# RWKV-7 recurrence of a two-network kernel: chunks of 64 tokens in place of chunks of 32

## Chip, core and metric

One core of one Trainium2 chip runs the whole program in one launch. The metric is the device time in microseconds (us). The kernel before takes 2678.37 us, the median of three runs (2671.02 to 2682.64).

## The reference, cut to what matters

Two small networks run one after the other on 256 latent and 256 context tokens of width 1024. Most of the work is matrix products with weights that stream from HBM. The change is in one part of the first network, the RWKV-7 recurrence of its even mixer: 8 heads of 64 features, two directions, and in each direction the 256 context tokens come first and hand their final state to the 256 latent tokens.

```
def step(S, inp):                       # S: [heads, 64 values, 64 keys]
    r, w, k, v, kk, a = inp             # one token
    S = (S * w[:, :, None, :]
         - jnp.einsum('bhvk,bhk->bhv', S, kk)[..., None] * (kk * a)[:, :, None, :]
         + v[..., None] * k[:, :, None, :])
    return S, jnp.einsum('bhvk,bhk->bhv', S, r)
S, y = lax.scan(step, S0, xs, reverse=reverse)
```

Token by token this is 512 dependent steps. In chunks it becomes products: inside a chunk the term in `kk` couples each token to the earlier ones, which needs the inverse of a triangular matrix 1 + N (N strictly triangular, as wide as the chunk) for each head and direction; between chunks only the state S is handed on.

## The kernel before

Names: d is the direction, m one of four pairs of heads, par the head within a pair, J a block of work. Features stand on partitions, so a pair of heads fills 128 partitions, 64 for each head.

`features` (L815) makes, for all tokens, `ARw` (alpha, rho: what multiplies the state) and `BKw` (kappa, beta: what goes into it), each with the decay from the chunk's start, and `EC`, the decay over the chunk before. It runs beside the global attention and ends at 664.9 us. Then the recurrence goes in 8 blocks of two chunks of 32 tokens, for both directions at once.

`prepare(J)` (L909) does what needs no state: products G of `BKw` and `ARw` (L922); N is cut from them (L928) and masked (L933); the causal mask gives the lower half of `AR` (L941), and `ARw` times the decay its upper half (L963); `BKw` is transposed to `TM` (L946, L950). Then the inverse `Z` of all 32 triangles (two directions, four pairs, four quadrants of 32 partitions for head and chunk) is made in two levels of three steps each, a step being 32 products of 32x32 blocks (L976) and one or two VectorE operations for each direction (L979 to L995). `Z` is written at L995.

`chain(J)` (L1001) takes the two chunks of the block one after the other. A tile `VS` holds for each head the state on its own 64 partitions and V and U on the other 64, so one product over all 128 partitions does for state and chunk together: R = `AR` (alpha) on `VS` (L1015), copied to `rs` (L1017); U = `Z` times `rs` (L1021), copied to `VS` in four pieces, in turns on VectorE and ScalarE (L1024); the new state from `TM` and V, U (L1028), plus the decayed old one (L1034, L1035); and the outputs Y (L1040), copied or added to `rt` (L1045, L1047).

`weave` runs `chain(J)` and two steps of `prepare(J + 1)` in turns, and a scheduler then sets the order in each engine's queue. A queue is taken in that order: an instruction that waits holds up all behind it. The last block is woven with the output projection (`ending`, and `out_split`).

All of these products are float32 and use part of TensorE's 128x128 array: the trace writes the part as rows*columns (64*64, 128*64, 32*32), and `tile_position` in the code says where in the array it stands. The trace shows two records for each such product, one for a transposing product.

Of the kernel before, what the change touches and what calls it, by code (L numbers as in the profile page):

```python
# [17 lines left out]
KD = 8  # L18
# [20 lines left out]

def weave_first(gen, *gens):  # L40
    """all in turns until the first has ended"""
# [6 lines left out]
def every(gen, n):  # L48
    """n steps of gen for one"""
# [5 lines left out]
def until(gen, mark):  # L55
    """the steps of gen as far as the mark; gen can go on from there"""
# [6 lines left out]
class Banks:  # L63
    """pools as one: their tiles in turns"""
# [10 lines left out]
class Net:  # L75
    def __init__(self, es, tc, ins, out):
# [7 lines left out]
        self.hp = p("h", 1)  # the normed stream while a phase multiplies it, other things of its size after  # L84
# [6 lines left out]
    def setup(self):  # L91
# [18 lines left out]
        self.unit = self.const.tile([128, 2, 32], F32, name="unit")  # ones in the first column, in the second  # L110
# [21 lines left out]
    def ring(self, es, raw, split):  # L132
        """for the length of a phase, more of the tiles [128, 1024] that weights go through"""
# [4 lines left out]
    def wtile(self, tag, dt):  # L138
        """in turns from the rings that there are, by their lengths"""
# [11 lines left out]
    def wload(self, w, r0, kt, c0, n):  # L151
        """rows r0.. (kt tiles of 128), columns c0..c0+n of w as (high, low) [128, kt, n]"""
# [31 lines left out]
    def proj_steps(self, h, w, c0, ncols, n, done, r0=0, kt=KD, tok=slice(0, 512)):  # L184
        """done(m, psum [128, n]) for each 128 columns of h.T @ w[:, c0:c0+ncols], features on partitions"""
# [34 lines left out]
    def behind(self, gen, n=99):  # L220
        """n steps of products, on TensorE after what is there so far"""
# [4 lines left out]
    def proj_t_steps(self, h, w, c0, ncols, toks, done, kt=KD):  # L226
        """done(tile, psum [128, ncols]) for each 128 tokens, tokens on partitions"""
# [61 lines left out]
    def mod_steps(self, name, w, fixes, gain=None, start=0):  # L289
        """silu(c) @ w + b for both conditionings to M[name], in steps; fixes: {chunk: (mul, add)}"""  # L290
# [3 lines left out]
        for g in range(start, (nch_all + 3) // 4):  # L294
# [46 lines left out]
    def psum(self, es, a, n=1, m=1, x=0, side="left"):  # L341
        """the PSUM pools of a phase: banks for products, norms, modulation, other things"""
# [7 lines left out]
    def tick(self, n=1, left=99):  # L350
        """n steps of the modulation vectors; no group of columns is begun with less than 8 of them left"""
# [13 lines left out]
    def rstd(self, src, ngroups, ones, ntok, eps, dst, psp=None, scale=1.0):  # L365
        """dst [128 tokens, ntok/128, ngroups] = 1 / sqrt(scale * ones' sums of src [128, ntok] (or of several) over partitions + eps)"""
# [11 lines left out]
    def bcast(self, ps, src):  # L378
        """ps [128, 128 tokens] = src [128 tokens, 1] on every partition"""
# [1767 lines left out]
```

## Time and profile before

| | |
|---|---|
| median of 3 runs | 2678.37 us (2671.02 to 2682.64) |
| profiled execution: span | 2679.4 us; the page has no time around it |
| TensorE busy over the span | 2539.3 us (95%), weight loads 2079.3 us beside it |
| VectorE, ScalarE, GpSimd busy | 1764.7, 1016.9, 672.7 us |
| granted TensorE clock, mean | 0.961 of 2.4 GHz |
| recurrence, first G to last Y | 664.9 to about 918 us |

The share of busy time is over the whole program; what bounds a stage is read from the stage's own windows and waits. "PE" is TensorE, "PEld" its weight loads, DVE VectorE, ACT ScalarE, POOL GpSimd. PE's records are pipelined and overlap, so the distance from the start of one group to the start of the next is the cost of a group. The granted clock is 1.00 (2.4 GHz) or 0.50 (1.2 GHz); a mean between them is a mixture.

### The profile page before, as it was taken

Reading aid. Unit: us, or ns where it says so; the run is one execution under the profiler, and the core shown is the slowest. Engines: PE = TensorE matmul, PEld = TensorE weight load, DVE = VectorE, ACT = ScalarE, POOL = GpSimd, SP = SyncE. Lnnn points to the kernel's source line nnn. Section 1 sums busy time; section 2 is a strip of 40 time slices with the busy share of each in tenths; the row PEclk is TensorE's granted clock in tenths of the full one; section 3 lists DMA queues with packets and bytes.
Section 4 is the critical chain, followed back from the end, with each engine's and each line's share of the span. In section 5 each row is a group of like instructions: output and inputs, shape, how many; then the busy total and the mean of one; then the engine's idle time right before and its main releaser. Section 6 shows DMA issues by size and latency. Waiting matters only on the chain.

```text
span 2679.4 us, 47406 instructions
## 1 busy us (share of the span) xinstructions
PE 2539.3 (95%) x19372; PEld 2079.3 (78%) x19372; DVE 1764.7 (66%) x2852; ACT 1016.9 (38%) x1916; POOL 672.7 (25%) x665
## 2 busy tenths in 40 slices
PE   7999999998878999999999999999999999999898
PEld 5777789854666887777897777885999887569675
DVE  4967745467666676778586877377554652765885
ACT  3322225345223252222242122366534643645454
POOL 2420322033333143113243113230414120012331
PEclk9999999988787989999999999999999999899999
DMA  8756643100000265566555666241665231023312
GB/s 263 222 175 210 183 123 98 32 0 1 3 4 27 81 180 182 180 194 198 151 149 166 211 186 185 79 132 43 182 186 150 76 103 47 16 67 105 88 48 71
DMA packets 426505, 321.32 MB, mean 120 GB/s; under 512 B 16784, under 2 KB 400528, under 8 KB 426288
## 3 DMA queue, kind: packets, MB, share of 16 engines
q1 hardware_dynamic: 426288, 318.30, 40.5%
q8 instruction: 152, 2.49, 0.4%
q14 instruction: 65, 0.53, 0.1%
HBM read 317.21 MB, written 1.05 MB: 119 GB/s over the span
## 4 chain that ended last, share of the span: by engine, by line
PE 83%; DVE 10%; ACT 3%; issue 2%; DMA 1%; POOL 1%; DVEq 0%; ACTq 0%; SPq 0%; POOLq 0%
PE ps_ff L172 9%; PE ps_ff L173 9%; PE ps_ff L174 9%; PE ps_pr L172 7%; PE ps_pr L173 6%; PE ps_pr L174 6%; PE ps_fo L172 5%; PE ps_fo L173 5%; PE ps_fo L174 5%; PE ps_s L725 3%; PE ps_o L760 2%; PE ps_w L976 2%; PE ps_ptr L751 1%; PE ps_st L1028 1%; DVE wl L157 1%
## 5 line engine op out<-in xcount | busy, mean ns | idle before, releaser
L156 ACT CAST wh<-wr 128x1024 fp32r<-128x1024 f32 (+2 forms) x402 | 417.0, 1043 | 990.5 <-PE ps_ff L173 415.6
L157 DVE TENSOR_TENSOR wl<-wr,wh 128x1024 fp32r<-128x1024 f32 (+2 forms) x402 | 521.4, 1301 | 396.1 <-ACT wh L156 393.0
L172 PE MATMUL ps_ff<-h,wh 128*128 128x512 f32 (+1 forms) x1232 | 451.9, 367 | 0.5 <-ACT fu L536 0.5
L173 PE MATMUL ps_ff<-h,wh 128*128 128x512 f32 (+1 forms) x1232 | 451.1, 366 | 0.0
L174 PE MATMUL ps_ff<-h,wl 128*128 128x512 f32 (+1 forms) x1232 | 450.5, 366 | 0.6 <-DVE wl L157 0.6
L420 POOL TENSOR_SCALAR uh<-fu 128x512 fp32r<-128x512 f32 (+1 forms) x88 | 169.3, 1924 | 774.0 <-DVE fu L537 774.0
L174 PE MATMUL ps_pr<-h,wl 128*128 128x256 f32 (+2 forms) x920 | 305.8, 334 | 12.9 <-DVE wl L157 12.8
L172 PE MATMUL ps_pr<-h,wh 128*128 128x256 f32 (+2 forms) x920 | 305.7, 337 | 7.2 <-ACT wh L156 4.5
L173 PE MATMUL ps_pr<-h,wh 128*128 128x256 f32 (+2 forms) x920 | 305.6, 334 | 2.5 <-POOL h L457 1.5
L305 DVE SCALAR_TENSOR_TENSOR acc<-wr,csa,acc 128x1024 f32<-128x1024 f32 x224 | 296.8, 1365 | 3.9 <-DMA wr<-in_w_mod_dram 3.9
L172 PE MATMUL ps_fo<-uh,wh 128*128 128x512 f32 (+1 forms) x824 | 278.9, 340 | 0.0
L173 PE MATMUL ps_fo<-uh,wh 128*128 128x512 f32 (+1 forms) x824 | 278.7, 339 | 0.0
L174 PE MATMUL ps_fo<-uh,wl 128*128 128x512 f32 (+1 forms) x824 | 277.7, 338 | 0.0
L172 PEld LDWEIGHTS ps_ff<-h,wh 128*128 128x128 f32 x1232 | 231.6, 188 | 51.6 <-ACT wh L156 6.7
L174 PEld LDWEIGHTS ps_ff<-h,wl 128*128 128x128 f32 x1232 | 231.6, 188 | 42.2 <-DVE wl L157 1.0
L173 PEld LDWEIGHTS ps_ff<-h,wh 128*128 128x128 f32 x1232 | 231.7, 188 | 40.5
L174 PEld LDWEIGHTS ps_pr<-h,wl 128*128 128x128 f32 x920 | 177.4, 193 | 30.6 <-DVE wl L157 14.5
L172 PEld LDWEIGHTS ps_pr<-h,wh 128*128 128x128 f32 x920 | 176.9, 194 | 28.0 <-ACT wh L156 8.2
L173 PEld LDWEIGHTS ps_pr<-h,wh 128*128 128x128 f32 x920 | 177.5, 194 | 20.3 <-POOL h L457 2.2
L172 PEld LDWEIGHTS ps_fo<-uh,wh 128*128 128x128 f32 x824 | 155.0, 188 | 26.7 <-issue 8.4
L173 PEld LDWEIGHTS ps_fo<-uh,wh 128*128 128x128 f32 x824 | 155.0, 188 | 18.8 <-issue 0.8
L174 PEld LDWEIGHTS ps_fo<-uh,wl 128*128 128x128 f32 x824 | 154.9, 188 | 18.2
(615 smaller groups left out, 4335.4 us busy)
## 6 DMA issues: line engine op xcount, KB each, us to landing
wr<-in_ffn_in_dram SPq DMA_DIRECT2D x176, 512.0 KB, 4.6
wr<-in_w_mod_dram SPq DMA_DIRECT2D x144, 512.0 KB, 4.4
wr<-in_ffn_out_dram SPq DMA_DIRECT2D x88, 512.0 KB, 4.3
wr<-in_l_w_in_dram SPq DMA_DIRECT2D x55, 512.0 KB, 3.8
wr<-in_l_w_mod_dram SPq DMA_DIRECT2D x48, 512.0 KB, 4.3
wr<-in_even_w_in_dram SPq DMA_DIRECT2D x21, 512.0 KB, 4.1
wr<-in_l_w_out_dram SPq DMA_DIRECT2D x16, 512.0 KB, 4.1
wr<-in_even_w_out_dram SPq DMA_DIRECT2D x14, 512.0 KB, 4.1
```

The costliest lines, as they stand in the source:

```text
L156: a = nc.scalar.copy(hi[:, : kt * n], raw)
L157: b = nc.vector.tensor_tensor(lo[:, : kt * n], raw, hi[:, : kt * n].bitcast(F32), ALU.subtract)
L172: mm(ps, a[0], b[0], start=first, stop=False)
L173: mm(ps, a[0], b[1], start=False, stop=False)
L174: self.mm = mm(ps, a[1], b[0], start=False, stop=last)
L305: nc.vector.scalar_tensor_tensor(acc[i], v, cs[:, k, i:i + 1], acc[i], ALU.mult, ALU.add)
L420: nc.gpsimd.tensor_scalar(hi, src, 1.0, None, ALU.mult)
L725: nc.tensor.matmul(s, q(h, q0s[b]), k(h), start=True, stop=True)
L751: nc.tensor.transpose(tr[:, j * 128:(j + 1) * 128], e[:, j * 128:(j + 1) * 128], self.ident)
L760: nc.tensor.matmul(o[64 * par:64 * par + 64, :nq], v(2 * m + par, j), PT[m, par][:, j, :nq], start=j == 0, stop=j == nk - 1, tile_position ...
L976: nc.tensor.matmul(out(rw, b), lhsT[rw, cl], rhs(rw, cl), start=True, stop=True, tile_position=(32 * q, 32 * q))
L1028: nc.tensor.matmul(Sv[half[par], d, m], TM[h, ks[d], d, m], S[h, par, d, m], start=True, stop=True, tile_position=(64 * (1 - par), 64 * par))
```

## The change

The chunk has 64 tokens, a block is one chunk, and there are 8 of both. G is a product of 64x128 in place of two of 64x64. Its masked copy `GM` [128, d, m, par, 128] now holds, for one head on all 128 partitions, what V and U multiply; the decayed `ARw` is a tile of its own (`AS`, on GpSimd), and so is the state (`S`). A product that took state and V, U together is now two: one with `AS` and `S` over 64 partitions, one with `GM` and `VU` over 128. For R the second of them is issued ahead (`begin`), the first in the chain; for Y they alternate. Block 0 has no state and no `AS`. The inverse of the 64x64 triangle is joined from its two 32x32 inverses: with the off-diagonal block `NO`, two further sets of 16 products and four that copy the second half (L997 to L1015), with the result in `ZF`. The four pieces of U become two copies of 64 partitions, the state one addition of 128 partitions. What follows is the core of the diff, without most of the lines it removes, which stand above; in the rest comments are dropped, widths of 32 become 64, and tiles that the output projection reuses get other names.

```diff
+        order = [(d, m, par) for d in range(2) for m in range(4) for par in range(2)]
...
         def prepare(J, U):
...
+            for d in range(2):
+                G = [P("g", "ps_g", 2).rearrange("p (m t) -> p m t", m=4) for _ in range(2)]
+                for m in range(4):
+                    for par in range(2):
+                        rw = half[par]
+                        nc.tensor.matmul(G[par][:, m], BKw[d][m][rw, c[d]].rearrange("p a t -> p (a t)"),
+                                         ARw[rw, d, m, c[d]].rearrange("p a t -> p (a t)"), start=True, stop=True, tile_position=(64 * par, 0))
+                for par in range(2):
+                    nc.vector.tensor_tensor(GM[:, d, :, par], G[par], mgm[:, d].unsqueeze(1).to_broadcast([128, 4, 128]), ALU.mult)
                 yield
+            for k in range(2):
+                for par in range(2):
+                    nc.scalar.copy(N[Q(2 * par + k)], GM[Q(2 + k), :, :, par, 32 * k:32 * k + 32])
...
+                    nc.gpsimd.tensor_copy(NO[Q(2 * par + k)], GM[Q(2 + k), d, :, par, 32 * (1 - k):32 * (1 - k) + 32])
...
+                nc.scalar.copy(TM[:, d], tr.rearrange("p (m f) -> p m f", m=4))
+                ck = c[d]
+                nc.gpsimd.memset(VU[64:128, d], 0.0)
+                nc.gpsimd.tensor_copy(VU[0:64, d].rearrange("p m x f -> p m (x f)"), vt[half[ck % 2], :, ck // 2 * 128:ck // 2 * 128 + 128])
+                if J:
+                    nc.gpsimd.tensor_tensor(AS[:, d], ARw[:, d, :, ck].rearrange("p m a t -> p m (a t)"),
+                                            EC[:, d, :, J:J + 1].to_broadcast([128, 4, 128]), ALU.mult)
...
+            for d in range(2):
+                nc.vector.transpose(ZT[:, 128 * d:128 * d + 128], f(Z)[:, 128 * d:128 * d + 128])
+            for d in range(2):
+                nc.gpsimd.tensor_scalar(ZF[:, d, :, first(d)], Z[:, d], hm[:, d:d + 1], None, ALU.mult)
...
+                        nc.tensor.matmul(WX[0][Q(b(d, par)), 32 * m:32 * m + 32], NO[Q(x), m], ZT[Q(x), 128 * d + 32 * m:128 * d + 32 * m + 32],
+                                         start=True, stop=True, tile_position=(32 * x, 32 * b(d, par)))
+            nc.scalar.copy(f(XT.unsqueeze(1)), WX[0][:, 0:128])
...
+                    nc.tensor.matmul(WX[d][Q(y), 256:384], eye[Q(y)], f(Z)[Q(y), 128 * d:128 * d + 128], start=True, stop=True, tile_position=(32 * y, 32 * y))
...
+                        nc.tensor.matmul(WX[d][Q(x), 256 + 32 * m:288 + 32 * m], XT[Q(y), m], Z[Q(y), d, m], start=True, stop=True, tile_position=(32 * y, 32 * x))
+            for d in range(2):
+                nc.scalar.copy(ZF[:, d, :, 1 - first(d)], WX[d][:, 256:384].rearrange("p (m t) -> p m t", m=4))
+        def begin(U):
+            R = U["R"] = P("c", "ps_ru").rearrange("p (d m v) -> p d m v", d=2, m=4)
+            for d, m, par in order:
+                nc.tensor.matmul(R[half[par], d, m], U["GM"][:, d, m, par, 0:64], U["VU"][:, d, m, par], start=(d, m) == (0, 0) or "AS" not in U, stop="AS" not in U, tile_position=(0, 64 * par))
+        def chain(J, U, Un):
...
+                for d, m, par in order:
+                    rw = half[par]
+                    nc.tensor.matmul(R[rw, d, m], AS[rw, d, m, 0:64], S[rw, d, m], start=False, stop=(d, m) == (1, 3), tile_position=(64 * par, 64 * par))
+            rs = T("rs", [128, 2, 4, 64])
+            nc.vector.tensor_copy(rs, R)
+            up = [P(f"s{par}", "ps_u").rearrange("p (d m v) -> p d m v", d=2, m=4) for par in range(2)]
+            for d, m, par in order:
+                nc.tensor.matmul(up[par][64:128, d, m], Z[half[par], d, m].rearrange("p k t -> p (k t)"), rs[half[par], d, m], start=True, stop=True, tile_position=(64 * par, 64))
+            for par in range(2):
+                (nc.scalar.copy if par else nc.vector.tensor_copy)(VU[64:128, :, :, par], up[par][64:128])
...
+                    nc.tensor.matmul(st[half[par], d, m], TM[:, d, m, 64 * par:64 * par + 64], VU[:, d, m, par], start=True, stop=True, tile_position=(0, 64 * par))
...
+                    nc.gpsimd.tensor_tensor(se, S, EC[:, :, :, J:J + 1].to_broadcast([128, 2, 4, 64]), ALU.mult)
+                    nc.vector.tensor_tensor(Sn, se, st, ALU.add)
...
+            Y = P("s1", "ps_y").rearrange("p (d m t) -> p d m t", d=2, m=4)
+            for d, m, par in order:
+                if J:
+                    rw = half[par]
+                    nc.tensor.matmul(Y[rw, d, m], S[rw, d, m], AS[rw, d, m, 64:128], start=True, stop=False, tile_position=(64 * par, 64 * par))
+                nc.tensor.matmul(Y[half[par], d, m], VU[:, d, m, par], GM[:, d, m, par, 64:128], start=not J, stop=True, tile_position=(0, 64 * par))
...
+            g = [chain(J, U, Un), (prepare(J + 1, Un), 3)]
```

What stands on TensorE in the middle of a block's inverse, before: the first level's second and third steps (`ps_w`) with the state's products (`ps_st`) and the outputs (`ps_ru<-AR`) between them.

```order
L976 MATMUL ps_w<-N_6915,wl 32x32 x32
L1028 MATMUL ps_st<-VS_5115,TM 64x64 x14
L976 MATMUL ps_w<-wl,WT 32x2x32 x32
L1040 MATMUL ps_ru<-AR,VS_5115 64x32 x5
L976 MATMUL ps_w<-wl,WT 32x32 x32
L1040 MATMUL ps_ru<-AR,VS_5115 64x32 x10
```

And now, at the same place (`ps_y` are the outputs, L1058 with the state on 64*64 of the array, L1059 with V and U on 128*64):

```order
L967 MATMUL ps_w<-N_6379,wl 32x32 x32
L1045 MATMUL ps_st<-VU,TM 64x64 x16
L967 MATMUL ps_w<-wl,WT 32x2x32 x32
L1058 MATMUL ps_y<-AS,S 64x64
L1059 MATMUL ps_y<-GM,VU 64x64
L1058 MATMUL ps_y<-AS,S 64x64
L1059 MATMUL ps_y<-GM,VU 64x64
L1058 MATMUL ps_y<-AS,S 64x64
L967 MATMUL ps_w<-wl,WT 32x32 x32
L1059 MATMUL ps_y<-GM,VU 64x64
L1058 MATMUL ps_y<-AS,S 64x64
L1059 MATMUL ps_y<-GM,VU 64x64
```

The outputs of a chunk stood in runs of one kind; now two kinds stand in turns, 32 products in a block with the inverse's steps among them.

What VectorE does between a block's inverse (`Z`) and the next one's beginning (L937 before, L938 now), before:

```order
L995 SCALAR_TENSOR_TENSOR Z<-ps_w,wl 128x128 x2
L1047 TENSOR_TENSOR rt<-rt,ps_ru 128x4x32 x2
L941 TENSOR_TENSOR AR<-ps_g,c_em_mask 64x512 x2
L963 TENSOR_TENSOR AR<-ARw,EC 64x4x2x64 x4
L928 COPY wl<-ps_g 32x256
L1017 COPY rs<-ps_ru 128x256
L941 TENSOR_TENSOR AR<-ps_g,c_em_mask 64x512 x2
L937 TENSOR_TENSOR wl<-c_em_mask,N_6911 128x256
```

And now (L990 are the transposes for the join):

```order
L986 SCALAR_TENSOR_TENSOR Z<-ps_w,wl 128x128
L990 STREAM_TRANSPOSE wl<-Z 128x128
L1034 COPY rs<-ps_ru 128x512
L924 TENSOR_TENSOR GM<-ps_g,c_em_mask 128x4x128 x4
L1040 COPY VU<-ps_u 64x8x64
L938 TENSOR_TENSOR wl<-c_em_mask,N_6818 128x256
```

The eight operations on `AR` are four on `GM`, the copy `rs` that releases U stands ahead of them, and the copies that cut N out have gone to ScalarE.

## Rows read from the trace of the kernel before

**Rows 1.** The page's first line.

```profile
span 2679.4 us, 47406 instructions
```

**Rows 2.** Windows: stretch, length, busy time of PE, PEld, DVE, ACT, POOL, granted clock, DMA.

```profile
674.00:854.00 180.00, 152.13 (x4502) 128.67 (x4502) 119.20 (x283) 48.51 (x142) 60.75 (x94) 0.77 0.01 3
...
888.00:919.00 31.00, 29.21 (x383) 26.18 (x382) 20.80 (x35) 8.03 (x14) 4.17 (x4) 0.94 0.30 87
...
720.00:722.00 2.00, 0.04 (x2) 0.00 (x0) 1.96 (x4) 0.00 (x0) 0.00 (x0) 1.00 0.00 0
...
842.00:844.00 2.00, 2.00 (x22) 1.82 (x19) 1.78 (x3) 0.17 (x1) 0.00 (x0) 0.50 0.03 8
```

**Rows 3.** The line that writes `Z`: count, ns min/median/max, first and last start.

```profile
L995 DVE SCALAR_TENSOR_TENSOR Z<-ps_w,wl x16: 251/292/293, 696.8 to 887.5; 128x128 f32<-128x128 f32 x16
```

**Rows 4.** Timeline of DVE: start, length, instructions.

```profile
681.69 0.43 DVE L937 TENSOR_TENSOR wl<-c_em_mask,N 128x256 f32<-128x256 f32 x1
...
715.09 0.72 DVE L995 SCALAR_TENSOR_TENSOR Z<-ps_w,wl 128x128 f32<-128x128 f32 x2 [0.78 <-PE ps_w L976]
```

**Rows 5.** Groups by line, 674 to 854 us: busy, mean ns, idle before.

```profile
L1034 POOL TENSOR_TENSOR se<-VS,EC 64x512 f32<-64x512 f32 x22 | 23.2, 1055 | 75.4 <-DVE VS L1035 73.2 <-DVE VS L1037 1.4
L956 POOL COPY VS<-vt 32x256 f32<-32x256 f32 x51 | 22.1, 433 | 3.9 <-PE ps_ru L1040 1.3
...
L941 DVE TENSOR_TENSOR AR<-ps_g,c_em_mask 64x512 f32<-64x512 f32 x28 | 19.3, 689 | 2.6 <-ACT wl L928 1.2 <-PE ps_ru L1040 0.9
L963 DVE TENSOR_TENSOR AR<-ARw,EC 64x512 f32<-64x512 f32 x24 | 19.0, 793 | 0.2
...
L1035 DVE TENSOR_TENSOR VS<-se,ps_st 64x512 f32<-64x512 f32 x20 | 13.7, 685 | 15.4 <-PE ps_st L1028 15.2
...
L1024 DVE COPY VS<-ps_u 32x256 f32<-32x256 f32 x24 | 10.1, 419 | 7.2 <-ACT VS L1024 3.5 <-PE ps_u L1021 2.2 <-PE ps_w L976 1.2
...
L1017 DVE COPY rs<-ps_ru 128x256 f32<-128x256 f32 x12 | 5.1, 422 | 5.9 <-PE ps_ru L1015 5.8
```

**Rows 6.** Nearest forms by line: DVE from PSUM, POOL, both of 128x512.

```profile
L1073 DVE TENSOR_TENSOR ycs<-ycs,ps_yr x4: 680/688/689, 813.0 to 928.2; 128x512 f32<-128x512 f32 x4
...
L866 POOL TENSOR_TENSOR t<-t,kk x8: 1262/1384/2292, 568.7 to 626.3; 128x512 f32<-128x512 f32 x8
```

**Rows 7.** Timeline of PE from 699.2 us, at full clock.

```profile
699.34 0.33 PE L1028 MATMUL ps_st<-VS,TM 64*64 64x64 f32 x2
699.60 0.30 PE L1040 MATMUL ps_ru<-AR,VS 128*64 128x32 f32 x2
699.83 0.33 PE L976 MATMUL ps_w<-N,wl 32*32 32x32 f32 x16
...
700.60 1.02 PE L1028 MATMUL ps_st<-VS,TM 64*64 64x64 f32 x26
701.56 0.31 PE L1040 MATMUL ps_ru<-AR,VS 128*64 128x32 f32 x4
```

**Rows 8.** Timeline of PE from 750.4 us, at half clock.

```profile
750.55 0.47 PE L1028 MATMUL ps_st<-VS,TM 64*64 64x64 f32 x2 [0.32 <-DVE VS L1024]
750.95 0.42 PE L1040 MATMUL ps_ru<-AR,VS 128*64 128x32 f32 x2
751.29 0.44 PE L976 MATMUL ps_w<-N,wl 32*32 32x32 f32 x16
```

**Rows 9.** Timeline of PE from 740 us, full clock: runs of one kind.

```profile
740.48 0.85 PE L976 MATMUL ps_w<-wl,WT 32*32 32x32 f32 x64 [0.72 <-DVE WT L987]
741.26 0.77 PE L1040 MATMUL ps_ru<-AR,VS 128*64 128x32 f32 x18
...
743.03 0.65 PE L1015 MATMUL ps_ru<-VS,AR 128*32 128x64 f32 x32
743.62 0.56 PE L922 MATMUL ps_g<-ARw,wr 64*64 64x64 f32 x12
744.02 0.51 PE L922 MATMUL ps_g<-ARw,wh 64*64 64x64 f32 x10
```

More of the change, by code (lines that the diff above doesn't have):

```diff
@@ L891, in rwkv @@
         Q = lambda b: slice(32 * b, 32 * b + 32)
-        VS = [T(f"VS{i}", [128, 2, 2, 4, 64]) for i in range(4)]
-        qz = lambda par, k: 2 * par + k
+        first = lambda d: d
+        order = [(d, m, par) for d in range(2) for m in range(4) for par in range(2)]
         def turn_v():
             for i, t in enumerate((2, 3, 0, 1)):
-                nc.vector.memset(VS[i], 0.0)
                 sl = slice(128 * t, 128 * t + 128)
@@ L937, in prepare @@
             nc.vector.tensor_tensor(ZM[:, 0].rearrange("p (x t) -> p x t", t=32), eye.unsqueeze(1).to_broadcast([128, 8, 32]), n1.rearrange("p d m t -> p (d m) t"), ALU.subtract)
-            for k in range(2):
+            yield
+            for d in range(2):
                 for par in range(2):
-                    rw = half[1 - par]
-                    nc.vector.tensor_tensor(AR[rw, par, k], Gv[k][rw], mgm[rw].unsqueeze(2).to_broadcast([64, 2, 4, 64]), ALU.mult)
-                yield
+                    k = first(d)
+                    nc.gpsimd.tensor_copy(NO[Q(2 * par + k)], GM[Q(2 + k), d, :, par, 32 * (1 - k):32 * (1 - k) + 32])
             for d in range(2):
@@ new lines, in prepare @@
+            for d in range(2):
+                nc.vector.transpose(ZT[:, 128 * d:128 * d + 128], f(Z)[:, 128 * d:128 * d + 128])
+            for d in range(2):
+                nc.gpsimd.tensor_scalar(ZF[:, d, :, first(d)], Z[:, d], hm[:, d:d + 1], None, ALU.mult)
+            WX = [P("w", "ps_w", 2) for _ in range(2)]
+            XT = T("XT", [128, 4, 32])
+            a = lambda d, par: 2 * par + first(d)
+            b = lambda d, par: 2 * par + 1 - first(d)
+            for m in range(4):
@@ L1022, in chain @@
                 for d in range(2):
                     for par in range(2):
-                        (nc.scalar.copy if par else nc.vector.tensor_copy)(S[Q(3 - 2 * par), par, d], up[Q(qz(par, ks[d]))])
-                yield
-                for d, m, par in order if pos < 15 else ():
-                    h = half[1 - par]
-                    nc.tensor.matmul(Sv[half[par], d, m], TM[h, ks[d], d, m], S[h, par, d, m], start=True, stop=True, tile_position=(64 * (1 - par), 64 * par))
-                if 0 < pos < 15:
-                    se = T("se", [128, 2, 4, 64])
@@ L1031, in chain @@
-                for par in range(2) if pos < 15 else ():
-                    rw = half[par]
-                    if pos:
-                        nc.gpsimd.tensor_tensor(se[rw], S[rw, par], EC[rw, :, :, pos:pos + 1].to_broadcast([64, 2, 4, 64]), ALU.mult)
-                        nc.vector.tensor_tensor(Sn[rw, par], se[rw], Sv[rw], ALU.add)
-                    else:
-                        nc.vector.tensor_copy(Sn[rw, par], Sv[rw])
-                yield
-                for d, m, par in order:
-                    nc.tensor.matmul(Y[half[par], d, m], S[:, par, d, m], AR[:, par, ks[d], d, m, 32:64], start=True, stop=True, tile_position=(0, 64 * par))
@@ L1041, in chain @@
-                for d in range(2):
-                    ck = c[d] + ks[d]
-                    yo = rt[:, :, 32 * ck:32 * ck + 32]
-                    if pos % 8 < 4:
-                        nc.scalar.copy(yo, Y[:, d])
-                    else:
-                        nc.vector.tensor_tensor(yo, yo, Y[:, d], ALU.add)
+                        x = a(d, par)
+                        nc.tensor.matmul(WX[0][Q(b(d, par)), 32 * m:32 * m + 32], NO[Q(x), m], ZT[Q(x), 128 * d + 32 * m:128 * d + 32 * m + 32],
+                                         start=True, stop=True, tile_position=(32 * x, 32 * b(d, par)))
@@ new lines, in chain @@
+        def chain(J, U, Un):
+            GM, TM, VU, Z, R = (U[n] for n in ("GM", "TM", "VU", "Z", "R"))
+            c = C0(J)
+            S = U.get("S")
+            if J:
+                AS = U["AS"]
+                for d, m, par in order:
[3 more added lines that the diff above has]
+            nc.vector.tensor_copy(rs, R)
+            yield
+            up = [P(f"s{par}", "ps_u").rearrange("p (d m v) -> p d m v", d=2, m=4) for par in range(2)]
+            for d, m, par in order:
+                nc.tensor.matmul(up[par][64:128, d, m], Z[half[par], d, m].rearrange("p k t -> p (k t)"), rs[half[par], d, m], start=True, stop=True, tile_position=(64 * par, 64))
+            for par in range(2):
+                (nc.scalar.copy if par else nc.vector.tensor_copy)(VU[64:128, :, :, par], up[par][64:128])
+            yield
+            if J < 7:
+                st = P("s0", "ps_st").rearrange("p (d m v) -> p d m v", d=2, m=4)
+                for d, m, par in order:
+                    nc.tensor.matmul(st[half[par], d, m], TM[:, d, m, 64 * par:64 * par + 64], VU[:, d, m, par], start=True, stop=True, tile_position=(0, 64 * par))
+                Sn = Un["S"] = T("S", [128, 2, 4, 64], 2)
+                if J:
+                    se = T("se", [128, 2, 4, 64])
+                    nc.gpsimd.tensor_tensor(se, S, EC[:, :, :, J:J + 1].to_broadcast([128, 2, 4, 64]), ALU.mult)
+                    nc.vector.tensor_tensor(Sn, se, st, ALU.add)
+                else:
+                    nc.vector.tensor_copy(Sn, st)
+                yield
+            Y = P("s1", "ps_y").rearrange("p (d m t) -> p d m t", d=2, m=4)
+            for d, m, par in order:
+                if J:
+                    rw = half[par]
+                    nc.tensor.matmul(Y[rw, d, m], S[rw, d, m], AS[rw, d, m, 64:128], start=True, stop=False, tile_position=(64 * par, 64 * par))
+                nc.tensor.matmul(Y[half[par], d, m], VU[:, d, m, par], GM[:, d, m, par, 64:128], start=not J, stop=True, tile_position=(0, 64 * par))
+            for d in range(2):
+                yo = rt[:, :, 64 * c[d]:64 * c[d] + 64]
+                if J % 4 < 2:
+                    nc.scalar.copy(yo, Y[:, d])
+                else:
+                    nc.vector.tensor_tensor(yo, yo, Y[:, d], ALU.add)
+            yield
+            if J < 7:
+                begin(Un)
@@ L1102, in ending @@
         def ending():
-            yield from zip_longest(chain(7, U), readout(span(64), "t"))
+            yield from zip_longest(chain(7, U, None), readout(span(64), "t"))
             yield from readout(ends, ("t", "c", "s0", "s1"))
@@ L2078, in layout @@
         lev += [u, u.T]
-    mask = np.tile(np.concatenate(tri + lev + [s_ == t_], axis=1).astype(np.float32), (4, 1)).reshape(2, 2, 32, -1)
-    for d in range(2):
-        mask[:, 1, :, 64 * d:64 * d + 32] = 0
-    A["em_mask"] = f(mask.reshape(128, -1))
+    A["em_mask"] = f(np.concatenate([tri, np.tile(np.concatenate(lev + [s_ == t_], axis=1).astype(np.float32), (4, 1)), np.arange(128)[:, None] // 32 % 2 == np.arange(2)[None, :]], axis=1).astype(np.float32))
     A["even_w_in"], A["even_w_out"] = f(g1("even_w_in")), f(g1("even_w_out"))
```

106 lines of the change are left out of this document (34 added, 72 removed).

## Prediction

> **What bounds the kernel now.** I read the page first [rows 1], then windows over the recurrence, the line that writes `Z` as a clock of its rounds, the groups by line inside it, and last the timeline of TensorE, where the products change their kind.
>
> The span is 2679.4 us and the page has no time around it [rows 1], 1 us above the median of the runs shown, so I add to 2679.4. The change is confined to the recurrence: `features` keeps its operations (fewer small copies of decay), and the phases behind it are bound by TensorE and simply begin earlier or later.
>
> `Z` is written 16 times, two for each of 8 blocks, from 696.8 to 887.5 us [rows 3]; the second block's stands at 715.1 [rows 4]. So there is a start of 32 us (664.9 to 696.8), a first round of 18.3 us, six rounds that take 172 us, 28.7 each, and an end in which the last chunks run among the output projection's products. Between 674 and 854 us TensorE is busy for 152.1 of 180 us and VectorE for 119.2, at a mean clock of 0.77 [rows 2]. Neither is full. With 0.5 and 1.0 as the only levels, 0.77 means half clock for 46% of the time. TensorE's idle 27.9 us are 4.2 us for each of the 6.6 rounds of 27.2 us (190.7 us by 7) in that stretch. The reader is to see the pattern at 720 us: TensorE does nothing for 2 us while VectorE is busy for 1.96 [rows 2], and the clock falls after it. VectorE's block there is the eight operations on `AR`; so the round is VectorE's block, then TensorE at half clock.
>
> **The change on TensorE.** Prices are distances from start to start, at full clock; a product leaves two records.
> - Now, for two chunks: G 32 products at 0.067 us (743.62 to 744.02, six) 2.1; R and U 32 each at 0.037 (743.03 to 743.62, sixteen) 2.4; the state's 32 at 0.074 (700.60 to 701.56, thirteen) 2.4; Y 32 at about 0.08 (nine in 0.77) 2.6 [rows 7, 9]. Sum 9.5 us.
> - New, all but Y: G 16 products with twice the columns in weight and moving operand, between 0.067 and four times that; I take 0.134: 2.1 us. `begin`, R, U and the state 16 each, 64-column runs of one kind, as the state's now: 64 by 0.074, 4.7 us. The join has 32 products of 32x32 at 0.024 (740.48 to 741.26, thirty-two) and four of four times the columns at 0.1: 1.2 us [rows 7, 9].
> - New, Y: L1058 (64\*64) and L1059 (128\*64) in turns. This is where I expect the change to be decided. A single product of one kind between others is not 0.07 us: at 699.34 one 64\*64 product takes 0.26 us until the next kind starts, at 699.60 one 128\*64 product 0.23, while thirteen of one kind take 0.96 [rows 7]. At half clock the two are 0.40 and 0.34 [rows 8]. The 128\*64 rows have 32 moving columns, the new product 64, so it lies between 0.23 and the 0.26 of the 64-column row; I take 0.255. Sixteen pairs at 0.515 are 8.2 us, at half clock (0.78) 12.5 us, against 2.6 now.
>
> Sum 16.2 against 9.5. Elsewhere the kind changes less often: in the order, from first G to last Y, it changes 246 times now and 407 times then, 213 of these between the two kinds of Y, so the others fall by 52, some 6 in a block, at 0.18 us each; a part is already in the prices, and I take off 0.7. That leaves +6.0 us of TensorE a round at full clock. At half clock Y adds 9.9 less its present 2.6 once more, the other groups double on both sides, and it is about +8.7. At 46% half clock: +7.2.
>
> What counts as a change of kind matters for the join, whose blocks stand off the diagonal of the array. G's neighbours stand in different places of the array too (tile positions 0, 64 and 64, 0), at 0.067 us each [rows 9], so I charge place nothing. The Trainium skill (TensorEngine Tiling (Array Packing), Key Properties) says that a change of tiling mode, not of the tile alone, drains TensorE. By that rule the join costs the 1.2 us above; were the place to count too, its 36 products at 0.25 would be 9 us, 47 us more in six rounds. The trace agrees with the rule at G's row; no row shows a 32x32 product off the diagonal.
>
> **On VectorE, GpSimd and ScalarE.** VectorE loses, in a block, four operations of 0.689 us (L941), four of 0.793 (L963), four of 0.685 (L1035), four of 0.419 (L1024), two of 0.422 (L1017): 11.2 us [rows 5]. It gains four masks, a state addition, `rs` and half of U, seven of 128x512 or 64x512 from PSUM at 0.688 [rows 6], and two transposes of about 0.3 (the 128x128 row of `Z` has 0.29 [rows 3]): 5.4 us. So 5.8 us less, of 18 a round, and no block of eight. The state's path is walked once in a round, not twice, and `rs` stands ahead of the masks. GpSimd loses eight copies of 0.433 and four products of 1.055, 7.7 us [rows 5]; it gains three of 1.38 (`AS` twice, `se`) [rows 6] and small copies, memsets and scalings which I put at 0.2 to 0.87 by the copy's row, 4 us in all: 8.1 us. Of these `ZF` and `NO`, about 2 us, stand ahead of the next masks of N; the 2.75 us of `GM` on VectorE hide them, and without that cover they cost 2 us by six rounds, 12 us. ScalarE gains two copies and has the time.
>
> TensorE's waits therefore shrink: of 4.2 us idle a round I leave 1, between the masks of G and the next inverse, where N has to pass ScalarE, GpSimd and VectorE in turn. That gives 3.2 us back. Below, nothing more than 4.2 can come from there; above, nothing may come back.
>
> **The sum.** Six rounds: +7.2 - 3.2 = +4.0 each, +24 us. The first round has no `AS`, its Y is of one kind and it needs no new R: TensorE saves about 1.4 us, I take -2 for the round. The start: VectorE's first mask for the inverse stands at 681.7 [rows 4] and `Z` comes 15 us later; now the six steps stand together in TensorE's queue, at four times 0.78 and twice about 1 us, with some 0.75 us of VectorE between, 9.5 us. With four memsets of `VS` gone as well I take -8, bounded by 0 and -14. The end: TensorE is busy for 29.2 of 31 us there [rows 2], so products count in full: 6 us of two chunks become U 1.2 and Y 8.2, +4 with some half clock. 24 - 2 - 8 + 4 = +18: 2697 us.
>
> **Rivals.**
> - *The clock stays up: faster.* Today's round holds 13.2 us at half clock, 84.5% busy; at full clock it would be 5.6 us shorter, 23.1. With +6.0 and -3.2 the new round is 25.9, -2.8 by six, -17; with -2, -8 and +3 the total is -24: 2655. Its place is the six rounds, its price 14.8 us for the whole round going from full to half clock, and it decides where the rounds' mean clock is above about 0.87 (29.7 us a round, the break-even with the -6 of the other parts). For it: the idle stretch that precedes the fall at 720 us [rows 2] goes. Against it: from 842 to 844 us TensorE is busy all the time and has half clock [rows 2], so busy is not enough, and the turns of Y are the emptiest kind of busy. The Trainium skill (TensorE: Matmul & The Clock Gate, Why this matters for your kernels) advises to keep TensorE continuously busy to have the full clock; by that rule this rival is what happens, 2655. The trace disagrees at 842 us, which lowers it, not to nothing. 0.18.
> - *The waits rule the round and hide the turns of Y: faster.* The round then falls with VectorE and the state's path, by up to the 5.8 us and the block before `rs`: 28.7 to 22, -40, -10 and +3: 2632. Against it: the turns stand between the inverse's own steps in TensorE's queue, where a step has under 1 us of VectorE to hide in. 0.09.
> - *The clock stays down: slower still.* If the turns of Y hold it at half for 90% of a round, it is 25.9 + 13.3 = 39.2, +63 - 6: 2736. For it: 842 us again. 0.18.
>
> **Numbers.** The forecast's case has 0.55, its own range is 2680 to 2715. This measurement can't tell less than 0.5%, 13.4 us, from no change: 2665 to 2691.8. Of the forecast's case some 0.38 is above that, 0.16 within, 0.01 below; the first rival gives 0.14 faster and 0.04 same, the second 0.09 faster, the third 0.18 slower. Faster 0.24, same 0.20, slower 0.56. The range leaves out the second rival, a little of the first and the far half of the third: 2650 to 2738.
>
> **What would show it.** In the profile after: L1058 and L1059 starting about 0.25 us apart at full clock and 0.4 at half; L1059's group among the costliest of the stage; VectorE's busy time in a round near 12 us and TensorE idle for about 1; rounds of `Z` (L986) of 31 to 34 us from the second on; the first `Z` 8 us nearer to the first G; the join's 36 products in about 1.2 us. The forecast is wrong if a pair of Y costs 0.2 us, if the rounds' mean clock is above 0.87 or far below 0.77, or if TensorE waits for something new, GpSimd's queue ahead of the masks first of all.

## The result and the profile after

The changed kernel takes 2699.65 us (median of six runs, 2696.0 to 2710.73) against 2675.0 (2671.02 to 2682.64): ratio 1.0078, interval 1.0052 to 1.0104. It is slower by 0.8%, and 2697 was forecast. The page's first line, which answers [rows 1]:

```profile
span 2694.7 us, 46752 instructions
```

The stage in parts, as windows whose borders are the same events in both kernels: first G, first `Z`, second block's `Z`, seventh block's `Z`, and the first group of four in the norm that follows (L449, VectorE). The second of the five windows is one round, the third holds five rounds, and the fourth the last round and the end. Columns as in [rows 2]. Before:

```profile
664.90:696.80 31.90, 23.48 (x613) 19.50 (x612) 24.90 (x48) 11.25 (x30) 13.60 (x22) 0.79 0.01 3
696.80:715.10 18.30, 16.10 (x610) 13.87 (x613) 10.55 (x32) 4.36 (x14) 7.50 (x11) 0.83 0.02 4
715.10:859.70 144.60, 122.02 (x3612) 103.46 (x3604) 95.80 (x228) 36.39 (x106) 47.36 (x73) 0.79 0.01 3
859.70:957.80 98.10, 85.56 (x1377) 77.89 (x1364) 67.25 (x123) 37.18 (x74) 26.39 (x28) 0.91 0.37 103
957.80:2679.40 1721.60, 1660.41 (x10091) 1384.51 (x10090) 1136.54 (x1827) 697.26 (x1297) 411.45 (x383) 0.98 0.44 129
```

After:

```profile
664.90:691.60 26.70, 22.83 (x563) 18.72 (x567) 11.54 (x30) 9.41 (x22) 13.87 (x22) 0.99 0.01 3
691.60:709.20 17.60, 15.22 (x605) 13.31 (x597) 8.64 (x27) 3.31 (x11) 5.91 (x11) 0.73 0.02 5
709.20:854.90 145.70, 138.61 (x3459) 111.46 (x3448) 64.20 (x169) 31.34 (x84) 49.15 (x79) 0.86 0.01 3
854.90:970.10 115.20, 106.25 (x1354) 94.17 (x1344) 58.17 (x105) 36.16 (x69) 23.65 (x28) 0.82 0.31 89
970.10:2694.70 1724.60, 1664.70 (x10091) 1387.15 (x10090) 1134.13 (x1827) 696.23 (x1297) 410.80 (x383) 0.98 0.45 129
```

The start is 5.2 us shorter, the first round 0.7; the five rounds behind it are 1.1 us longer in all, the last round with the end 17.1, and what follows 3.0. That is the 15.3 us between the spans. The medians are 24.65 us apart: the profiled span of the kernel before (2679.4) lies above its median time, that of the changed kernel (2694.7) below. So the parts explain 15.3 us, from one execution of each. In the five rounds TensorE's idle time falls from 22.6 to 7.1 us, VectorE's busy time by a third, and the clock rises from 0.79 to 0.86; TensorE is busy for 16.6 us more. In the last part the clock falls, from 0.91 to 0.82.

The line that writes `Z` ends later now, to be set beside [rows 3]; and the stretch of [rows 2] has 15 us more of TensorE and 38 less of VectorE:

```profile
L986 DVE SCALAR_TENSOR_TENSOR Z<-ps_w,wl x16: 251/261/292, 691.6 to 896.6; 128x128 f32<-128x128 f32 x16
```

```profile
674.00:854.00 180.00, 167.22 (x4459) 135.90 (x4458) 80.78 (x219) 39.66 (x107) 61.61 (x102) 0.86 0.01 3
```

Y's two kinds, two rows that were not there before (groups by line, 674 to 854 us; durations overlap), and then the timeline of TensorE at full and at half clock, which answers [rows 7, 8]:

```profile
L1059 PE MATMUL ps_y<-GM,VU 128*64 128x64 f32 x192 | 32.2, 270 | 0.1
L1058 PE MATMUL ps_y<-AS,S 64*64 64x64 f32 x160 | 29.7, 273 | 0.0
```

```profile
786.06 0.33 PE L1058 MATMUL ps_y<-AS,S 64*64 64x64 f32 x2
786.32 0.33 PE L1059 MATMUL ps_y<-GM,VU 128*64 128x64 f32 x2
786.58 0.32 PE L1058 MATMUL ps_y<-AS,S 64*64 64x64 f32 x2
...
882.20 0.47 PE L1059 MATMUL ps_y<-GM,VU 128*64 128x64 f32 x2
882.61 0.47 PE L1058 MATMUL ps_y<-AS,S 64*64 64x64 f32 x2
883.01 0.47 PE L1059 MATMUL ps_y<-GM,VU 128*64 128x64 f32 x2
```

From start to start a product takes 0.26 us at full clock and 0.405 at half. Windows of 2 us over Y of another block show the clock falling:

```profile
844.00:846.00 2.00, 2.00 (x73) 1.55 (x59) 0.61 (x2) 0.53 (x2) 0.00 (x0) 1.00 0.00 0
846.00:848.00 2.00, 2.00 (x18) 1.50 (x16) 0.00 (x0) 0.00 (x0) 0.00 (x0) 1.00 0.00 0
848.00:850.00 2.00, 2.00 (x12) 1.43 (x10) 0.00 (x0) 0.00 (x0) 0.00 (x0) 0.51 0.00 0
```

By the profile TensorE is busy without a gap for the 4 us ahead of 848 us, and the clock falls there all the same. A step of the inverse (`ps_w`) ran until 844.4 us, and nothing but Y's turns from there to the fall.

### The profile page after: what moved, and what is told of

The parts are those of the page before. It is cut to its first block, busy times and chain, and to the rows that moved or that the text cites. A ratio compares the mean times of both kernels' runs of the same rounds, so it can differ in the third digit from the quotient of the medians.

```text
span 2694.7 us, 46752 instructions
## 1 busy us (share of the span) xinstructions
PE 2578.5 (96%) x19116; PEld 2104.6 (78%) x19116; DVE 1706.2 (63%) x2753; ACT 1006.2 (37%) x1876; POOL 671.2 (25%) x669
## 3 DMA queue, kind: packets, MB, share of 16 engines
HBM read 317.27 MB, written 1.05 MB: 118 GB/s over the span
## 4 chain that ended last, share of the span: by engine, by line
PE 84%; DVE 9%; ACT 3%; issue 2%; DMA 1%; POOL 1%; DVEq 0%; ACTq 0%; SPq 0%; POOLq 0%
PE ps_ff L172 9%; PE ps_ff L173 9%; PE ps_ff L174 9%; PE ps_pr L172 7%; PE ps_pr L173 7%; PE ps_pr L174 7%; PE ps_fo L172 5%; PE ps_fo L173 5%; PE ps_fo L174 5%; PE ps_s L725 2%; PE ps_o L760 2%; PE ps_w L967 2%; PE ps_y L1059 1%; PE ps_y L1058 1%; PE ps_ptr L751 1%
## 5 line engine op out<-in xcount | busy, mean ns | idle before, releaser
L156 ACT CAST wh<-wr 128x1024 fp32r<-128x1024 f32 (+2 forms) x402 | 417.0, 1043 | 1018.6 <-PE ps_ff L173 400.5
L172 PEld LDWEIGHTS ps_fo<-uh,wh 128*128 128x128 f32 x824 | 155.0, 188 | 26.7 <-issue 8.4
```

Source lines behind the costliest of these rows:

```text
L156: a = nc.scalar.copy(hi[:, : kt * n], raw)
L172: mm(ps, a[0], b[0], start=first, stop=False)
```

## The experiments

All but two start from the changed kernel and alter the loop of Y (or what is said). The kind of a product is the part of the array that it uses (64\*64 or 128\*64), its place is where that part stands, and products are in turns when each one is of another kind than the one before. The first two have one edit, with n = 16 (two runs) and n = 4 (fours), and twos are n = 2:

```diff
-            for d, m, par in order:
-                if J: (state's product)
-                (V and U's product)
+            for i in range(0, 16, n):
+                if J:
+                    for d, m, par in order[i:i + n]:
+                        rw = half[par]
+                        nc.tensor.matmul(Y[rw, d, m], S[rw, d, m], AS[rw, d, m, 64:128], start=(d, m) == (0, 0), stop=False, ...)
+                for d, m, par in order[i:i + n]:
+                    nc.tensor.matmul(Y[half[par], d, m], VU[:, d, m, par], GM[:, d, m, par, 64:128], start=not J, ...)
```

With the order the flag that starts a sum changes too: it was set for each of the state's products, and is now set for the first of each head only.

**Two runs.**

> The changed kernel with Y's products in two runs: all 16 of the state (L1058), then all 16 of V and U (L1059). Theory T (the turns of Y are the price): a pair falls from 0.515 us to 2 x 0.074, 16 pairs give 5.9 us a block at full clock, about 6.8 at the clock of these rounds (0.86), seven blocks 47 us; TensorE's waits take back 5 to 15 us: 2657 to 2667 us, and fewer falls of the clock in the middle of Y. Rival W (the waits rule the round): TensorE idles for what it saves, less than 12 us comes back: 2688 or above. Rival C (idle time lowers the clock): the products shrink as in T, but the mean clock of the five middle rounds goes back from 0.86 to 0.79 or below: about 2675.

Measured: 2644.99 us (2638.76 to 2650.12), ratio to before 0.9872 (0.9827 to 0.9918): 55 us less than with the turns, and faster than before. Rivals W and C fall; T's mechanism holds, but T allowed for a gain of 33 to 43 us only. The products and the parts of the stage (same borders):

```profile
793.00 0.68 PE L1059 MATMUL ps_y<-AS,S 64*64 64x64 f32 x16
793.62 1.15 PE L1061 MATMUL ps_y<-GM,VU 128*64 128x64 f32 x32
794.70 0.48 PE L967 MATMUL ps_w<-wl,WT 32*32 32x64 f32 x20
```

```profile
664.90:689.60 24.70, 22.45 (x554) 18.63 (x555) 11.60 (x29) 8.87 (x20) 13.88 (x22) 0.95 0.01 4
...
707.00:823.40 116.40, 103.09 (x3479) 87.44 (x3467) 64.73 (x171) 31.93 (x86) 49.95 (x80) 0.94 0.02 4
823.40:916.80 93.40, 83.48 (x1311) 77.68 (x1310) 55.64 (x103) 35.50 (x68) 21.30 (x27) 0.91 0.38 109
```

Sixteen products of a run take 1.08 us. Against the turns the five rounds lose 29.3 us, 35.5 of busy time less 6.2 that come back as idle. A block's Y in turns is 16 by 0.52, 8.3 us, in two runs 2.2; seven blocks make 43 us at full clock by this estimate. With the idle time that comes back, some 18 us of the 55 are left for the clock: it goes up to 0.94, and the last part has 0.91 again.

**Fours, twos.**

> The changed kernel with Y's products in groups of four of one kind (four of the state, four of V and U, and so on): 7 changes of kind within a block's Y in place of 31. Theory T: the gain goes with the changes that are taken out, 24 of the 30 that two runs take out, so 0.8 of that experiment's gain: 2664 to 2674 us; the first product of each four takes 0.25 us to the next, the other three 0.074. Rival (a product's price is set by its own shape, or by each switch between accumulating and starting, not by the change of shape): the start-to-start distance stays 0.257 for all 32, no gain: 2700.

> The changed kernel with Y's products in twos of one kind. From the distances measured at full clock (a single one 0.257 us, a four 0.38, a run of sixteen 1.08) a product that follows one of its kind adds 0.04 to 0.06, so a two takes about 0.30 us and the 16 of them 4.8 us, against 8.2 in turns, 3.0 in fours and 2.2 in two runs: of the 6.0 us of full clock between the ends 57% are gone. If the time goes with it: 2666 to 2672 us. If the low clock of the turns goes with it too: 2650 to 2660. If only the number of changes counted (15 in place of 31): 0.52 of the gain, 2671 us.

Fours: 2642.82 us (2639.31 to 2645.66), 0.9857 (0.9819 to 0.9896), no slower than two runs. Twos: 2650.64 (2646.28 to 2657.2), 0.9883 (0.9855 to 0.991). So the gain doesn't go with the number of changes: with 15 of 31 left, nine tenths of it is there. The timelines, fours and then twos:

```profile
791.83 0.45 PE L1059 MATMUL ps_y<-AS,S 64*64 64x64 f32 x8
792.21 0.45 PE L1061 MATMUL ps_y<-GM,VU 128*64 128x64 f32 x8
792.59 0.45 PE L1059 MATMUL ps_y<-AS,S 64*64 64x64 f32 x8
```

```profile
716.80 0.33 PE L1059 MATMUL ps_y<-AS,S 64*64 64x64 f32 x4
717.07 0.34 PE L1061 MATMUL ps_y<-GM,VU 128*64 128x64 f32 x4
717.33 0.33 PE L1059 MATMUL ps_y<-AS,S 64*64 64x64 f32 x4
```

From start to start a four takes 0.38 us, not the 0.47 that its expectation adds up to, and a two 0.265: no more than a single product. The two heads of a two stand in different places of the array.

**Twos and runs in one place.** The same products, ordered so that a two holds one head's place only, and two runs with first one head's eight, then the other's:

```diff
+            tiles = [(d, m, par) for d in range(2) for m2 in (0, 2) for par in range(2) for m in (m2, m2 + 1)]   # twos
+            tiles = sorted(order, key=lambda x: x[2])                                                            # runs
```

> As the kernel with Y's products in twos of one kind, but the two products of a two are of the same head's place in the array (par equal) and not of the two places side by side. In the twos before a two took 0.264 us, no more than a single product (0.257). Theory P (neighbours of one kind in different places of the array run side by side, and the turns lose that as well as they pay for the change): a two in one place takes 0.37 to 0.39 us, Y 6.1 us a block in place of 4.2, seven blocks 13 us and more at the lower clock: 2662 to 2680 us. Rival D (only the change costs, and what follows in the same kind is hidden in it): 0.26 us again, 2646 to 2657 us.

> As the kernel with Y in two runs of 16, but within a run first the eight products of the one place (par 0), then the eight of the other. Theory P: products of one place follow at about 0.12 us in place of 0.067, so Y takes 4 us a block in place of 2.2, seven blocks 13 us, of which TensorE's waits (2.7 us a round) hide some: 2648 to 2660 us. Rival D: 0.067 us each as before, 2638 to 2650 us.

```profile
744.17 0.44 PE L1060 MATMUL ps_y<-AS,S 64*64 64x64 f32 x4
744.54 0.45 PE L1062 MATMUL ps_y<-GM,VU 128*64 128x64 f32 x4
744.92 0.44 PE L1060 MATMUL ps_y<-AS,S 64*64 64x64 f32 x4
```

```profile
796.73 1.90 PE L1062 MATMUL ps_y<-GM,VU 128*64 128x64 f32 x32
798.56 0.65 PE L967 MATMUL ps_w<-wl,WT 32*32 32x64 f32 x32
```

The prices are P's: a two in one place takes 0.375 us, and in a run a product of one place 0.114 (1.83 by 16) against 0.067. The times of the whole kernel say less. Twos in one place: 2660.16 us (2652.71 to 2664.95), 0.9905 (0.9868 to 0.9942), 2 us below P's range and 3 above D's; runs by place: 2646.65 (2642.32 to 2648.43), 0.9852 (0.9813 to 0.9892), in D's range and 1 below P's. Neither time can be told from that of the same groups in two places: the intervals overlap. The five rounds can, twos in one place first:

```profile
705.00:836.80 131.80, 124.43 (x3462) 104.36 (x3448) 64.32 (x169) 31.34 (x84) 47.85 (x77) 0.88 0.01 3
```

```profile
707.60:826.10 118.50, 109.23 (x3481) 94.24 (x3469) 64.08 (x170) 31.89 (x86) 49.80 (x80) 0.94 0.02 4
```

Twos in two places take 123.0 us there, with TensorE busy for 114.7, so in one place the price is paid in full, 8.8 us. The runs by place have 6.1 us more of TensorE than the two runs above but are 2.1 us longer: 4.0 us come out of idle time. An estimate from these distances: of the 0.19 us that a product in turns takes beyond its 0.067, two thirds are the change itself, 0.13 us (0.265 for a two less 0.135 for two products of a run), and one third is the neighbour that it could have run beside.

**In turns, but of one kind.** The state is kept with zeros on the other head's partitions, so that both products of Y are 128\*64 and still alternate:

```diff
-  S[rw, d, m], AS[rw, d, m, 64:128], ..., tile_position=(64 * par, 64 * par)
+  S[:, d, m, par], AS[:, d, m, 64:128], ..., tile_position=(0, 64 * par)
```

> The changed kernel with Y's products still in turns, but all of one shape, 128*64: the state is kept for each head with zeros on the other head's 64 partitions, so the state's product also runs over 128 partitions (the state is written in two VectorE and two GpSimd operations of 64 partitions in place of one each of 128; ZF has one buffer, the decayed state is made in place). Theory T (it is the change of shape that costs): 32 products about 0.075 us apart, 2.4 us for Y as in two runs; the state's path is about 1 to 2 us longer a round: 2660 to 2675 us. Rival A (what costs is to go back and forth between two pairs of operands or between starting and adding to a sum in PSUM): the products stay 0.25 us apart, and with the longer path of the state 2705 to 2715 us.

```profile
796.96 0.33 PE L1063 MATMUL ps_y<-AS,S 128*64 128x64 f32 x4
797.07 0.34 PE L1064 MATMUL ps_y<-GM,VU 128*64 128x64 f32 x4
797.19 0.34 PE L1063 MATMUL ps_y<-AS,S 128*64 128x64 f32 x4
```

2647.15 us (2644.58 to 2649.74), 0.9874 (0.9836 to 0.9912), and four products in 0.23 us. In the code the products alternate as before, with the same flags; in the trace they start by twos (x4 is two products, one for each head). Such a two takes 0.115 us, where a two of changing shape took 0.265. The price is gone: rival A falls, the change of shape is the cause.

**The old kernel with turns.** Control: before, with Y's loop moved right behind the state's. Test: the two in turns in one loop.

```diff
+                for d, m, par in order:
+                    h = half[1 - par]
+                    if pos < 15:
+                        (state's product, L1028)
+                    (Y's product, L1040)
```

> The kernel before with Y's 16 products of a chunk (L1040) moved right behind the 16 of its state (L1028), in two runs of one kind each; nothing else. All theories: the same work, only the place of Y in TensorE's queue moves, so within 10 us of before: 2665 to 2690 us. It is the control for the next one.

> The kernel before with the state's products (64*64) and Y's (128*64) of a chunk in turns, as the changed kernel has them within Y; the same products as in the control. Theory T (the turns, not the chunk of 64, are the price): 15 chunks with 16 pairs, each 0.49 us in place of 0.154 at full clock (0.74 in place of 0.30 at half): 5.4 to 7 us a chunk, 80 to 105 us in all, of which waits of today (4.2 us a round) can hide up to 30: 50 to 105 us above the control, and the clock falls within the turns. Rival (the turns cost in the changed kernel only, since there both products add to the same sum in PSUM): no more than 10 us above the control.

```profile
733.30 0.32 PE L1029 MATMUL ps_st<-VS,TM 64*64 64x64 f32 x2
733.55 0.30 PE L1030 MATMUL ps_ru<-AR,VS 128*64 128x32 f32 x2
733.78 0.33 PE L1029 MATMUL ps_st<-VS,TM 64*64 64x64 f32 x2
```

Control 2688.22 us (2673.94 to 2698.89), 1.0013 (0.9988 to 1.0038): no difference that shows. Turns 2797.94 (2790.06 to 2802.52), 1.0427 (1.0397 to 1.0457), 110 us above it, a little over T's range. From the first to the last `Z` the clock is 0.65, the control's 0.73, so a part of the 110 us is the clock. The turns cost in a kernel with chunks of 32 as well, where the two products do not add to one sum.

**What the chunk of 64 gains once the turns are gone.** Two runs, and VectorE's work or the path of the state made as long as they were: masks of G done three times, copies of rs and U done three times, and both.

```diff
-                for par in range(2):
+                for par in (0, 1, 0, 1, 0, 1):
                     nc.vector.tensor_tensor(GM[:, d, :, par], G[par], ...)
...
+            for _ in range(3):
                 nc.vector.tensor_copy(rs, R)
-            for par in range(2):
+            for par in (0, 1, 0, 1, 0, 1):
                 (nc.scalar.copy if par else nc.vector.tensor_copy)(VU[64:128, :, :, par], up[par][64:128])
```

> The changed kernel with Y in two runs, and each of the four masks of G in a block done three times over (the same result), which gives VectorE 8 operations of 0.685 us, 5.5 us, back at the place where the kernel before had its eight operations on AR. Theory V (the gain of the chunk of 64, once the turns are gone, is VectorE's work gone from ahead of the chain, and with the waits the low clock): TensorE's idle time grows by 2 to 5 us a round and the mean clock of the five middle rounds falls from 0.94 towards 0.80: 2660 to 2685 us. Rival (VectorE has room, the five rounds are TensorE's): at most 1 us a round, clock unchanged: 2645 to 2652 us.

> The changed kernel with Y in two runs, and the copies on the path from R to the new state done three times each (rs, and U's two copies; the same results): the path is walked about 2.8 us later a round (two more copies of 0.69 for rs, two of 0.69 or 0.58 for U), about as if the state passed twice as many copies, as in the kernel before. Theory S (the gain of the chunk of 64 without the turns is the path of the state, walked once in place of twice): TensorE's idle time grows by 2 to 3 us a round, in eight rounds 16 to 24 us: 2660 to 2670. Rival (TensorE has the next block's inverse to do meanwhile): under 1 us a round, 2645 to 2652.

> The changed kernel with Y in two runs, the path of the state longer by 2.8 us a round as in the kernel with copies done three times, and the masks of G done three times as in the one that gives VectorE 5.5 us a block back. If VectorE's work and the path of the state make up what the chunk of 64 gains, this is back at the kernel before, 2670 to 2690 us; if the two add without more, 15 us for the masks and what the path alone costs; if neither is the cause, under 2665.

Masks: 2659.58 us (2653.08 to 2661.72), 0.9906 (0.9876 to 0.9936), 15 above two runs by the times and 9 by the ratios, whose intervals overlap. Path: 2644.78 (2637.57 to 2646.99), 0.988 (0.9842 to 0.9917), no difference that shows. Both: 2679.18 (2669.82 to 2691.01), 0.9999 (0.9981 to 1.0018), 34 above two runs. The five rounds of the three, one fence each:

```profile
714.50:842.35 127.85, 112.63 (x3451) 95.13 (x3450) 87.65 (x210) 32.15 (x86) 49.96 (x80) 0.92 0.02 4
```

```profile
704.40:823.60 119.20, 105.13 (x3514) 87.93 (x3512) 77.89 (x193) 37.82 (x96) 49.81 (x80) 0.97 0.02 4
```

```profile
717.00:857.50 140.50, 123.97 (x3482) 103.20 (x3479) 100.91 (x230) 38.18 (x96) 49.87 (x80) 0.81 0.01 3
```

Theory V hit the size of the masks' cost nearly, but not how: idle grows from 13.3 to 15.2 us in five rounds, 0.4 a round, the clock stays at 0.92, and the start alone is 6.6 us longer. Theory S falls only in part, since that edit lengthened the path by less than its expectation says. U waits for `ZF`, which the join writes, and the added copies of `rs` end before it:

```profile
751.43 2.10 DVE L1035 COPY rs<-ps_ru 128x512 f32<-128x512 f32 x3
757.70 1.15 PE L1039 MATMUL ps_u<-rs,ZF 64*64 64x64 f32 x32 [0.20 <-ACT ZF L1015]
```

What was tried is some 2 us more between the first product of U and the first of the state (1.9 to 2.6 us in two runs, 4.5 to 4.7 here, in the five rounds), and these cost nothing that shows. Only with both does the stage look like before's, VectorE busy for 100.9 of 140.5 us (before 95.8 of 144.6) and the clock at 0.81 (0.79). So these two together are enough to undo the whole gain. That the gain comes from them is not shown by this, as VectorE then has more work than before; and which step brings the clock down was not tried.

## Why the prediction was right, and where it was not

- *The turns of Y.* Right in place, kind and size: 0.515 us a pair forecast, 0.52 measured, 0.78 and 0.81 at half clock; shown by the two runs, by the kernel of one kind and by the old kernel with turns. The reason was half told: the prediction charged the change of kind and did not see that neighbours in two places run side by side.
- *The join.* Its products fill 0.18, 0.50 and 0.60 us of the round at 766 us, about 1.3 against 1.2. To change the place costs nothing here, as was assumed; to stay in one place is what costs (0.114 for 0.067 above).
- *The new operations.* The mask of G takes 685 ns, as its nearest row [rows 6] had it (688); `AS` and `se` on GpSimd take 1.05 us, not the 1.38 taken from there; the old `se` [rows 5] had 1.055. Groups by line, 674 to 854 us:

```profile
L924 DVE TENSOR_TENSOR GM<-ps_g,c_em_mask 128x512 f32<-128x512 f32 x24 | 15.5, 685 | 14.8 <-PE ps_g L921 8.3 <-PE ps_y L1059 6.5
L953 POOL TENSOR_TENSOR AS<-ARw,EC 128x512 f32<-128x512 f32 x10 | 10.3, 1047 | 56.5 <-PE ps_y L1058 56.5
...
L1049 POOL TENSOR_TENSOR se<-S,EC 128x512 f32<-128x512 f32 x6 | 6.3, 1057 | 21.9 <-DVE S L1050 15.4 <-DVE S L1052 6.5
```

- *TensorE's waits.* -3.2 us a round forecast; 22.6 to 7.1 us in five rounds is -3.1. VectorE's busy time went from 19.2 to 12.8 us a round, some 6 less, where 5.8 were forecast. GpSimd's queue did not become a wait in these rounds.
- *The failed step: "at 46% half clock: +7.2" a round.* Measured are +3.3 of busy time in the five rounds, so they came out at +1.1 in all, not +20. Busy time multiplied by the granted clock is an estimate of the work: 122.0 by 0.79 is 96.4 us, 138.6 by 0.86 is 119.2, so 4.6 us a round and not 6.0. It counts the turns low where the clock is at half (0.405 by 0.5 is 0.2, not 0.26). So the larger miss is the clock: I carried its share over from before, and it rose to 0.86, the border of the first rival (0.87). Both things that this rival names, fewer idle stretches and a higher clock, were there in these rounds, and the falls within Y took a part back (two runs have 0.94). That the one brings the other is not shown: two runs idle for 13.3 us and have the higher clock.
- *The last round and the end: +17.1, forecast +8.* The work is 9.2 us more by the same estimate (77.9 to 87.1) and idle time 3.6 less, so the rest of the 17 is the clock, 0.91 to 0.82. It falls at 868.5 us, ahead of the turns and in the second of two waits that the prediction did not have: the state's products stand for 2.4 and 2.9 us until U's two copies are done, and ScalarE's copy stood behind three casts of the output projection's weights (L156), the first of which had waited for its transfer.

```profile
869.18 1.55 PE L1045 MATMUL ps_st<-VU,TM 128*64 128x64 f32 x24 [2.88 <-ACT VU L1040]
```

  Two runs have the same waits, 2.8 and 2.7 us, and fall likewise, but are back at full clock 10 us later; with the turns it is at half for 24 us, over all of this block's Y (882 us above); the last block's Y is at half from 913 us on, its middle. No run takes these waits away.
- *The start.* -5.2, forecast -8: from the first mask (681.0) the inverse took 10.6 us to `Z`, not 9.5, and the mask came 0.7 earlier. One profile says little here: two runs, fours and twos, with the same work in this stretch, took 24.7, 24.0 and 20.2 us for the 26.7. First round -0.7, forecast -2. These rows answer [rows 4]:

```profile
680.97 0.41 DVE L938 TENSOR_TENSOR wl<-c_em_mask,N 128x256 f32<-128x256 f32 x1
...
691.56 0.29 DVE L986 SCALAR_TENSOR_TENSOR Z<-ps_w,wl 128x128 f32<-128x128 f32 x1 [0.98 <-PE ps_w L967]
```

- *The sum.* 2697 against 2699.65, but the rounds were 19 us under their terms and the last part 9 over, the start and the first round 4, and 3 us came behind the stage, where I had put none: its length was 1717 to 1725 us in the profiles, so that may be scatter. That the total was met so closely is luck: errors of 19 us and of 16 us cancel, and 2697 was added to the span 2679.4, not to the median. As a difference 18 us were forecast, 15.3 lie between the spans and 24.65 between the medians.
- *The second rival* (waits rule the round, 2632) is out for this kernel, with 1.4 us idle a round; without the turns idle is 2.7. *The third* (clock down for 90% of a round) is not seen: the lowest mean of a round is 0.71, in the last one.
- *The rule to keep TensorE busy* (the Trainium skill, TensorE: Matmul & The Clock Gate, Why this matters for your kernels): the windows at 844 to 850 us do not follow it, since the clock falls while TensorE is busy for 2.00 of 2.00 us by the profile.

## What to carry to other kernels

Look in the order of TensorE's queue for small products of two shapes in turns, and put them in groups of four or more of one shape, neighbours in different places of the array: here that took 55 to 57 us off and made a loss of 0.8% a gain of 1.4% (fours), with the same products. The price read at one place of the trace held at another here (0.515 and 0.52 us), the clock did not: a forecast that carries today's share of half clock into a changed stage should carry a range for it. When a stage's edits are put back one at a time, do the pair too: one cost 9 to 15 us, the other none, both 34. And look in the trace whether an edit that is to lengthen a path does so: copies ahead of a wait that ends later lengthen nothing.

## What the runs showed that was not expected

- Behind a change of shape, two 64-wide products in different places of the array take 0.265 us, a single one 0.26, two in one place 0.375. The Trainium skill (TensorEngine Tiling (Array Packing), Key Properties) says that different tiles can work in parallel; these rows agree, and show that a change of shape ahead of each product gives it away.
- In four of the five middle rounds the granted clock fell in the middle of Y's turns. In three of these falls (755.9, 817.3 and 848.0 us) TensorE was busy for 2.00 of 2.00 us in the windows of the 4 us ahead; ahead of the other, at 725.1, it had idled for 1.0 us. With the same products in two runs the mean of these rounds was 0.94, for 0.86.
